# Output units of a two-layer hybrid decoder without overlap, and the last one in two halves of 256 columns

## The chip, the cores and the metric

The kernel runs on one core of one Trainium2 chip. The metric is the device time of one execution in microseconds (us); lower is better. The core's engines are named as in the profile: PE (TensorE matmul), DVE (VectorE), ACT (ScalarE), POOL (GpSimd) and SP (SyncE, which issues nearly all transfers).

## What is computed

Two layers run over one sequence of 512 tokens of width 1024, in float32. The reference, cut:

```python
def hybrid_layer(x, w_in, w_out, g_pre, g_post, lb, g_head, sinks):
    h = rms_norm(x, g_pre)
    proj = jnp.einsum('bsd,de->bse', h, w_in)                       # 1024 -> 6400
    q_h, f_h, i_h, z_h, q_a, k_a, v_a, z_a = jnp.split(proj, SPLIT_POINTS, axis=-1)
    o_h = hgrn2(q_h, f_h, i_h, lb)                                  # gated linear recurrence, 8 heads of 128
    o_h = rms_norm(o_h, g_head).reshape(B, S, HG_WIDTH) * jax.nn.silu(z_h)
    o_a = sliding_window_attention(rotary(q_a), rotary(k_a), v_a, sinks) * jax.nn.silu(z_a)
    y = jnp.einsum('bse,ed->bsd', jnp.concatenate([o_h, o_a], axis=-1), w_out)   # 2048 -> 1024
    return x + rms_norm(y, g_post)

def reference(x, ...):
    for l in range(DEPTH):                                          # DEPTH = 2
        x = hybrid_layer(x, w_in[l], w_out[l], ...)
    return x
```

The change is in the last lines of the layer: the product with `w_out`, the norm of its result `y`, and the sum with `x`. What follows in layer 0 is the norm at the start of layer 1.

## The kernel before

**Products and units.** Every large product is made of three matmuls, on operands split into a high and a low part (`whi`, `wlo` for weights; `hhi`, `hlo` for the normed input; `ops` for both parts of the gated branch outputs). `products` lists them. A *unit* (`Unit`) is one PSUM tile of a product, called `pj`, of 128 tokens (a *token tile*, `tt`, 0 to 3) by 512 columns. It has a number of steps, one per 128 rows of contraction, and each step is three matmuls (line 240). Three `pj` tiles exist.

**The order of units.** `enqueue` puts the units of a product in one queue, `units`, for both layers ahead of time; `step` issues one step. At most two units are active at a time, and their steps alternate: a second unit starts when the one active has at most half of its steps left. Only the key/value product (`fresh`) runs its units alone. When a unit has made its last step, its `evac` is called, which writes the instructions that take the result out of PSUM. `later` keeps work to be written a number of steps on; `ensure` writes it at once if a unit needs it.

**The output product.** Its weights come in four slabs: `a0`, `a1`, `h0`, `h1`, by 512 rows of the 2048. Each slab has 8 units, 4 token tiles by 2 column halves (`ch`) of 512, of 4 steps each. `wo_stream` queues them; the results of the four slabs are added up in the SBUF tiles `y` (line 786 for the first, line 789 for the others). The slab `h1` is the last of its layer, and its units go token tile by token tile. It follows the gate slab `ZH+1`, whose units have 8 steps; the transposes at line 770 turn that gate's result into `ops`.

**After the last product of a token tile** `final` runs. For column half 0: the square sum on ACT (line 819) and the product with `g_post` on POOL, in place (line 821). For column half 1: the square sum on ACT, the product with `g_post` on DVE (line 824, tile `s`), then `rstd2`: the two sums and a constant added on DVE (line 296), the power -1/2 on POOL (line 298, tile `r`); then for each half the scaling and sum with `x` on DVE (line 827, tile `a`) and the transfer from the SP queue (line 828), to `x_mid` in layer 0 and to the output in layer 1.

**The hand-over to layer 1.** In layer 0, `final` ends with `pre_norm`, the next layer's norm of that token tile: the squares of `a` on ACT (line 331, written to `hlo`), the weighing on DVE (`xg`, line 344), `rstd2` again, and a diagonal matrix of `r` on DVE (line 347, `z` in the profile). 18 steps later (`DEFER`) the transposes on PE against that diagonal (line 352) go into two of three PSUM tiles, `sc`, that take turns; ACT copies them out as `hhi` (line 357) and DVE as `hlo` (line 361). Layer 1's first product, keys and values (128 by 256 per unit), needs them.

**What sets the order.** The kernel's Python writes the instructions in one stream. A scheduler then places each engine's instructions by priority and dependence, so the order on an engine follows when work was written. Instructions wrapped in `pin`, and those under `tc.high_priority(200)` (the last additions into `y`), are treated apart. Within an engine the placed order is kept at run time.

Of the kernel before, what the change touches and what calls it, by code (L numbers as in the profile page):

```python
# [10 lines left out]
F32 = mybir.dt.float32  # L11
F32R = mybir.dt.float32r
U8 = mybir.dt.uint8
AF = mybir.ActivationFunctionType
ALU = mybir.AluOpType
# [5 lines left out]
NT = SEQ // 128  # L21
# [44 lines left out]
def hybrid_kernel(ctx: ExitStack, tc: tile.TileContext, x, wkv, win, wout, g_pre, g_post, lbp, ghead, sinks,  # L66
                  ident_c, cos_f, sin_f, cos_t, sin_t, masks_c, out):
    nc = tc.nc
    P = 128
# [5 lines left out]
    sm = ctx.enter_context(tc.tile_pool(name="sm", bufs=4))  # L75
# [6 lines left out]
    def pj():  # L82
        return ps.tile([P, 512], F32, tag="pj", name="pj", bufs=PJ)
# [8 lines left out]
    def ac():  # L92
        return ps.tile([P, 512], F32, tag="ac", name="ac", bufs=8 - PJ - SC)

    def tmp(tag, dt=F32, n=1):

        t = tp.tile([P, n, 512] if n > 1 else [P, 512], dt, tag=tag, name=tag, bufs=TB[tag])
        return t
# [6 lines left out]
    x_mid = dr.tile([SEQ, D_MODEL], F32, name="x_mid")  # L105
# [18 lines left out]
    for l in range(1, DEPTH):  # L124
        i = plan_order.index((l, "kv"))
# [35 lines left out]
    def w_conv(n):  # L161
        w_load(n)
        while state["conv"] < min(n, len(pieces)):
            i = state["conv"]
            if state["limit"] is not None and i >= state["limit"]:
                return
            if i in kv_pieces and kv_pieces[i] not in kv_room:
                return
            w_load(i + RAW_BUFS)
            v = raws.pop(i)  # L170
            if i in kv_pieces:
                hi, lo = (big.tile([P, 512], F32R, tag="v", name="wkv", bufs=8) for _ in range(2))
            else:
                hi = wp.tile([P, 512], F32R, tag="whi", name="whi")
                lo = wp.tile([P, 512], F32R, tag="wlo", name="wlo")
            keep = pin if i in in_turn else lambda ins: ins
            keep(nc.scalar.copy(hi, v))  # L177
            keep((nc.gpsimd if i in on_pool and i % 2 else nc.vector).tensor_tensor(lo, v, hi.bitcast(F32), op=ALU.subtract))  # L178
            conv[i] = (hi, lo)
            state["conv"] += 1  # L180
# [5 lines left out]
    def products(ks, fresh):  # L186
        if not fresh:
            return [(k, i, j) for k in ks for i, j in EACH]
        return [(k, i, j) for i, j in ((0, 0), (0, 1), (1, 0)) for k in ks]
# [8 lines left out]
    def run_first():  # L198
        _, key, fn = waiting.pop(0)
        fn()  # L200
        emitted.add(key)

    def ensure(key):
        while key not in emitted:
            run_first()
# [3 lines left out]
    class Unit:  # L209
        def __init__(self, key, ks, sta, mov, evac, needs, ncol):  # L210
            self.key, self.ks, self.sta, self.mov, self.evac, self.needs, self.ncol = key, list(ks), sta, mov, evac, needs, ncol
            self.i = 0
            self.fresh = key[0] == "kv"
            self.list = products(self.ks, self.fresh)

    units, active, turn, slab_steps, slab_done = deque(), [], [0], {}, {}

    def enqueue(key, specs, ncol=512):

        for ks, sta, mov, evac, needs in specs:  # L220
            units.append(Unit(key, ks, sta, mov, evac, needs, ncol))
            slab_steps[key] = slab_steps.get(key, 0) + len(units[-1].ks)
            slab_done.setdefault(key, 0)

    def step():
        if not active or (len(active) == 1 and units and not active[0].fresh and not units[0].fresh
                          and 2 * (len(active[0].ks) - active[0].i) <= len(active[0].ks)):
            u = units.popleft()
            first, n = slab_first[u.key]
            w_conv(first + n)  # L230
            u.w = [conv[first + j] for j in range(n)]
            for key in u.needs:
                ensure(key)
            u.o = pj()[:, 0:u.ncol]
            active.append(u)
        u = active[turn[0] % len(active)]
        turn[0] += 1
        for n in range(3 * u.i, 3 * u.i + 3):
            k, i, j = u.list[n]
            nc.tensor.matmul(u.o, lhsT=u.sta(k, u.w)[i], rhs=u.mov(k, u.w)[j], start=(n == 0), stop=(n == len(u.list) - 1))  # L240
        u.i += 1
        for e in waiting:
            e[0] -= 1
        while waiting and waiting[0][0] <= 0:
            run_first()
        slab_done[u.key] += 1
        first, n = slab_first[u.key]
        w_conv(ahead.get(u.key, first + n) + slab_done[u.key] * KT // slab_steps[u.key] + LEAD)
        if u.i == len(u.ks):
            active.remove(u)  # L250
            u.evac(u.o)
# [4 lines left out]
    def through(key):  # L256
        while slab_done[key] < slab_steps[key]:
            step()
            yield 1.0
# [41 lines left out]
    def halves(tag):  # L301
        t = tmp(tag, n=2)
        return [t[:, 0], t[:, 1]]

    def load_g(g):
        t = halves("b")
        for c in range(2):
            nc.sync.dma_start(t[c], g[c * 512:(c + 1) * 512].partition_broadcast(P))
        return t
# [70 lines left out]
    def diagonals():  # L380
        return tmp("z1").rearrange("p (n t) -> p n t", n=NT)

    def new_hT():
        return (hp.tile([P, KT, SEQ], F32R, tag="hhi", name="hhi"), hp.tile([P, KT, SEQ], F32R, tag="hlo", name="hlo"))


    def layer(l, last):
# [391 lines left out]
        yt = {}  # L779

        def wo_stream(b, s, final=None):
            def evac(o, tt, ch):
                if (b, s) == ("a", 0):
                    if ch == 0:
                        yt[tt] = big.tile([P, 2, 512], F32, tag="oy", name="y", bufs=6)
                    nc.scalar.copy(yt[tt][:, ch], o)
                else:
                    with tc.high_priority(200 if final else 0):
                        nc.vector.tensor_tensor(yt[tt][:, ch], o, yt[tt][:, ch], op=ALU.add)
                if final is not None:  # L790
                    final(tt, ch)

            enqueue(("out", l, f"{b}{s}"),
                    [(range(4 * ch, 4 * ch + 4), lambda k, w, tt=tt: tuple(t[:, k % 4, tt * P:(tt + 1) * P] for t in ops_t[b, s]),
                      lambda k, w: w[k], lambda o, tt=tt, ch=ch: evac(o, tt, ch), [("o", l, b, s, tt)])
                     for tt, ch in ([(tt, ch) for tt in range(NT) for ch in range(2)] if final else
                                    [(tt, ch) for ch in range(2) for tt in range(NT)])])


        hT2 = {}  # L800

        def final(tt, ch):
            if ch == 0:
                if tt == 0:
                    hT2["gpost"] = load_g(g_post[l])
                    if not last:
                        hT2["gpre"] = [ac() for _ in range(2)]
                        for c, t in enumerate(load_g(g_pre[l + 1])):
                            nc.scalar.copy(hT2["gpre"][c], t)
                        hT2["dg"] = diagonals()  # L810
                        state["limit"] = slab_first["in", l + 1, QA][0] + 2
                        hT[l + 1] = new_hT()
                hT2["x"] = halves("a")
                for c in range(2):
                    nc.sync.dma_start(hT2["x"][c], (x if l == 0 else x_mid)[tt * P:(tt + 1) * P, c * 512:(c + 1) * 512])
                hT2["ss"] = sm.tile([P, 2], F32, tag="ss", name="ss")
            xt, ss, y = hT2["x"], hT2["ss"], yt[tt]
            junk = tmp("u")
            nc.scalar.activation(junk, y[:, ch], AF.Square, scale=1.0 / 32.0, accum_out=ss[:, ch:ch + 1])
            if ch == 0:  # L820
                nc.gpsimd.tensor_tensor(y[:, 0], y[:, 0], hT2["gpost"][0], op=ALU.mult)
                return
            yg = tmp("s")
            nc.vector.tensor_tensor(yg, y[:, 1], hT2["gpost"][1], op=ALU.mult)
            r = rstd2(ss)
            for c, v in ((0, y[:, 0]), (1, yg)):
                nc.vector.scalar_tensor_tensor(xt[c], v, r, xt[c], op0=ALU.mult, op1=ALU.add)
                nc.sync.dma_start((out if last else x_mid)[tt * P:(tt + 1) * P, c * 512:(c + 1) * 512], xt[c])
            if not last:
                pre_norm(tt, xt, hT2["gpre"], hT[l + 1], ("h", l + 1, tt), hT2["dg"], DEFER)  # L830

# [72 lines left out]
    m, n = head[0], head[1]  # L904
# [141 lines left out]
```

## Time and profile before

| | |
|---|---|
| median of 3 runs | 951.08 us (949.64 to 951.56) |
| the profiled execution, its own time | 947.43 us |
| its span, first to last instruction | 945.3 us |
| granted TensorE clock | 0.998 |
| end of layer 0's last output product (last matmul starts) | 474.63 us |
| start of layer 1's first 512-column product | 493.76 us |
| last matmul starts | 937.07 us |
| last scaling on DVE starts | 941.32 us |

Times of instructions are counted from the span's start. Rows of the timeline give the start, the duration, the engine, the line of the code, the operation, and what is written from what; a bracket gives the engine's idle time ahead of it and what ended that. PE rows overlap, since a matmul's row reaches to its modelled end while the next already runs; the distance between starts is the pace. The tiles of one name are not told apart there (`s` is the tile at line 824 and also the small sum at line 296, told apart by 128x512 and 128x1).

### The profile page before, as it was taken

Reading aid. Unit: us, or ns where it says so; the run is one execution under the profiler, and the core shown is the slowest. Engines: PE = TensorE matmul, PEld = TensorE weight load, DVE = VectorE, ACT = ScalarE, POOL = GpSimd, SP = SyncE. Lnnn points to the kernel's source line nnn. Section 1 sums busy time; section 2 is a strip of 40 time slices with the busy share of each in tenths; the row PEclk is TensorE's granted clock in tenths of the full one; section 3 lists DMA queues with packets and bytes.
Section 4 is the critical chain, followed back from the end, with each engine's and each line's share of the span. In section 5 each row is a group of like instructions: output and inputs, shape, how many; then the busy total and the mean of one; then the engine's idle time right before and its main releaser. Section 6 shows DMA issues by size and latency. Waiting matters only on the chain.

```text
span 945.3 us, 19154 instructions
## 1 busy us (share of the span) xinstructions
PE 918.9 (97%) x7286; PEld 757.0 (80%) x7286; DVE 679.6 (72%) x1328; ACT 471.9 (50%) x1098; POOL 267.9 (28%) x285
## 2 busy tenths in 40 slices
PE   8999998999999999999999989989999999999996
PEld 6887787778878788788888877877787887887885
DVE  5787869796767685865776688778867668749546
ACT  4434656837464462334453266676463635415242
POOL 2232444422231221221222344433413213113102
PEclk9999999999999999999999999999999999999999
DMA  6475523132222333333445836123223233323313
GB/s 221 135 224 160 168 61 90 56 92 68 79 79 80 89 113 90 111 89 94 132 144 170 234 77 179 57 67 89 70 67 90 69 89 95 119 63 97 89 34 134
DMA packets 56432, 100.83 MB, mean 107 GB/s; under 512 B 6418, under 2 KB 8850, under 8 KB 56340
## 3 DMA queue, kind: packets, MB, share of 16 engines
q1 hardware_dynamic: 56192, 99.53, 35.7%
q8 instruction: 58, 0.95, 0.4%
q14 instruction: 34, 0.28, 0.1%
q10 hardware_dynamic: 148, 0.07, 0.0%
HBM read 87.00 MB, written 12.58 MB: 105 GB/s over the span
## 4 chain that ended last, share of the span: by engine, by line
PE 77%; DVE 10%; ACT 5%; issue 4%; POOL 2%; DMA 1%; SPq 0%; DVEq 0%; POOLq 0%; ACTq 0%
PE pj L240 64%; DVE wlo L178 3%; PE sc L653 2%; ACT s L512 2%; PE ac L722 2%; PE sc L498 1%; PE ac L710 1%; PE ac L551 1%; PE ac L725 1%; PE sc L352 1%; DVE oa L557 1%; ACT whi L177 1%; PE sc L770 1%; DVE mx L503 1%; DVE sc L502 1%
## 5 line engine op out<-in xcount | busy, mean ns | idle before, releaser
L177 ACT CAST whi<-raw 128x512 fp32r<-128x512 f32 x256 | 157.7, 620 | 183.6 <-PE pj L240 161.0
L178 DVE TENSOR_TENSOR wlo<-raw,whi 128x512 fp32r<-128x512 f32 x249 | 189.5, 767 | 56.3 <-ACT whi L177 54.4
L240 PE MATMUL pj<-hhi,wlo 128*128 128x512 f32 x512 | 205.5, 401 | 0.0
L240 PE MATMUL pj<-hhi,whi 128*128 128x512 f32 x512 | 200.0, 391 | 0.0
L240 PE MATMUL pj<-hlo,whi 128*128 128x512 f32 x512 | 199.7, 390 | 0.0
L240 PE MATMUL pj<-whi,ops 128*128 128x512 f32 x512 | 173.6, 398 | 0.0
L240 PEld LDWEIGHTS pj<-hhi,whi 128*128 128x128 f32 x512 | 96.1, 188 | 21.0
L240 PEld LDWEIGHTS pj<-whi,ops 128*128 128x128 f32 x512 | 96.1, 188 | 19.9
L240 PEld LDWEIGHTS pj<-hhi,wlo 128*128 128x128 f32 x512 | 96.2, 188 | 19.0
L240 PEld LDWEIGHTS pj<-hlo,whi 128*128 128x128 f32 x512 | 96.3, 188 | 18.2
L240 PE MATMUL pj<-whi,hlo 128*128 128x512 f32 x256 | 103.9, 406 | 0.0
L240 PE MATMUL pj<-whi,hhi 128*128 128x512 f32 x256 | 100.3, 392 | 0.0
L240 PE MATMUL pj<-wlo,hhi 128*128 128x512 f32 x256 | 100.2, 391 | 0.0
L240 PE MATMUL pj<-wlo,ops 128*128 128x512 f32 x256 | 99.7, 389 | 0.0
L671 POOL TENSOR_TENSOR k<-k,tot 128x256 f32<-128x256 f32 x80 | 65.2, 833 | 109.7 <-PE sc L653 64.3
L670 DVE TENSOR_TENSOR q<-q,tot 128x256 f32<-128x256 f32 x80 | 47.8, 625 | 15.6 <-PE sc L653 10.1
L512 ACT ACTIVATE s<-sc,negm 128x128 f32<-128x128 f32 x128 | 45.6, 369 | 25.0 <-DVE negm L506 22.9
L240 PEld LDWEIGHTS pj<-whi,hhi 128*128 128x128 f32 x256 | 48.1, 188 | 10.1
L240 PEld LDWEIGHTS pj<-wlo,ops 128*128 128x128 f32 x256 | 48.2, 188 | 9.0
L240 PEld LDWEIGHTS pj<-whi,hlo 128*128 128x128 f32 x256 | 48.2, 188 | 8.0
L519 POOL TENSOR_TENSOR s<-s,sums 128x512 f32<-128x512 f32 x32 | 33.4, 1043 | 74.5 <-DVE sums L517 37.6
L240 PEld LDWEIGHTS pj<-wlo,hhi 128*128 128x128 f32 x256 | 48.3, 189 | 7.7
(178 smaller groups left out, 1440.2 us busy)
## 6 DMA issues: line engine op xcount, KB each, us to landing
raw<-in_win_dram SPq DMA_DIRECT2D x192, 256.0 KB, 2.7
raw<-in_wout_dram SPq DMA_DIRECT2D x64, 256.0 KB, 2.7
stack<-rot SPq DMA_DIRECT2D x16, 512.0 KB, 4.6
qs<-stack SPq DMA_DIRECT2D x32, 256.0 KB, 4.9
a<-in_x_dram SPq DMA_DIRECT2D x12, 256.0 KB, 3.4
raw<-in_wkv_dram SPq DMA_DIRECT2D x8, 256.0 KB, 4.2
x_mid<-a SPq DMA_DIRECT2D x8, 256.0 KB, 3.4
a<-x_mid SPq DMA_DIRECT2D x8, 256.0 KB, 3.6
```

The lines of the kernel that those rows point to most:

```text
L177: keep(nc.scalar.copy(hi, v))
L178: keep((nc.gpsimd if i in on_pool and i % 2 else nc.vector).tensor_tensor(lo, v, hi.bitcast(F32), op=ALU.subtract))
L240: nc.tensor.matmul(u.o, lhsT=u.sta(k, u.w)[i], rhs=u.mov(k, u.w)[j], start=(n == 0), stop=(n == len(u.list) - 1))
L352: pin(nc.tensor.matmul(o[:, j * P:(j + 1) * P], lhsT=self.xg[:, c, j * P:(j + 1) * P], rhs=self.dg[:, self.tt], start=True, stop=True))
L498: pin(nc.tensor.matmul(S[:, h * 256:(h + 1) * 256], lhsT=q[:, 2 * hp_ + h, t_], rhs=kst[v][p][:, (n - 1) * P:(n + 1) * P], start=(h == 0 a ...
L502: nc.vector.copy_predicated(Sv[:, :, P:2 * P], am2, Sv[:, :, 0:P])
L512: nc.scalar.activation(pt[:, h * P:(h + 1) * P], cur[h], AF.Exp, bias=negm[:, h:h + 1], scale=SCALE, accum_out=sums[:, h:h + 1])
L519: nc.gpsimd.tensor_tensor(pv, pv, sums.unsqueeze(2).broadcast_to([P, 4, P]), op=ALU.mult)
L653: pin(nc.tensor.matmul(L[32 * b:32 * b + 32, c:c + 16], lhsT=k[:, o_:o_ + 32], rhs=qv[:, blk:blk + qu, 1, :], start=True, stop=True, tile_ ...
L670: nc.vector.tensor_tensor(qv[:, :, 1, :], qv[:, :, 1, :], tv[:, :, 0].unsqueeze(2).broadcast_to([P, nb, hh]), op=ALU.mult)
L671: nc.gpsimd.tensor_tensor(kv_[:, :, 0, :], kv_[:, :, 0, :], tv[:, :, 1].unsqueeze(2).broadcast_to([P, nb, hh]), op=ALU.mult)
L722: pin(nc.tensor.matmul(O[:, c], lhsT=A[:, c], rhs=vs(j, n), start=(n == 0), stop=False))
```

## The change

Units of the slab `h1`, of both layers, are `alone`, as the key/value units were: none starts beside them, and they start beside none. In the last layer the last unit of the slab (token tile 3, column half 1) is replaced by two units of 256 columns each. The additions into `y` and the square sums go by these halves; the sums of column half 0 and of the first 256 columns are added by one DVE instruction of one column, so that `rstd2` still adds two numbers. The last token tile's scaling goes in three parts (512, 256 and 256 columns), and the transfer of the second part is issued from ACT's queue, the others from SP's.

```diff
@@ class Unit
             self.fresh = key[0] == "kv"
+            self.alone = self.fresh or key[2] == "h1"
@@ def enqueue
-        for ks, sta, mov, evac, needs in specs:
-            units.append(Unit(key, ks, sta, mov, evac, needs, ncol))
+        for ks, sta, mov, evac, needs, *own in specs:
+            units.append(Unit(key, ks, sta, mov, evac, needs, own[0] if own else ncol))
@@ def step
-        if not active or (len(active) == 1 and units and not active[0].fresh and not units[0].fresh
+        if not active or (len(active) == 1 and units and not active[0].alone and not units[0].alone
                           and 2 * (len(active[0].ks) - active[0].i) <= len(active[0].ks)):
@@ def wo_stream
-                    with tc.high_priority(200 if final else 0):
-                        nc.vector.tensor_tensor(yt[tt][:, ch], o, yt[tt][:, ch], op=ALU.add)
+                    y = yt[tt][:, ch, c0:c0 + n]
+                    with tc.high_priority(200 if final else 0):
+                        nc.vector.tensor_tensor(y, o, y, op=ALU.add)
...
+            if final:
+                todo = [(tt, ch, 0, 512) for tt in range(NT) for ch in range(2)]
+                if last:
+                    todo[-1:] = [(NT - 1, 1, 0, 256), (NT - 1, 1, 256, 256)]
+            else:
+                todo = [(tt, ch, 0, 512) for ch in range(2) for tt in range(NT)]
@@ def final
-        def final(tt, ch):
+        def final(tt, ch, c0, n):
+            split = n < 512
...
+            if c0:
+                hT2["ss"] = sm.tile([P, 2], F32, tag="ss", name="ss")
+                nc.vector.tensor_tensor(hT2["ss"][:, 0:1], ss[:, 0:1], ss[:, 1:2], op=ALU.add)
+                ss = hT2["ss"]
             junk = tmp("u")
-            nc.scalar.activation(junk, y[:, ch], AF.Square, scale=1.0 / 32.0, accum_out=ss[:, ch:ch + 1])
+            nc.scalar.activation(junk[:, 0:n], y[:, ch, c0:c0 + n], AF.Square, scale=1.0 / 32.0, accum_out=ss[:, ch:ch + 1])
...
-            yg = tmp("s")
-            nc.vector.tensor_tensor(yg, y[:, 1], hT2["gpost"][1], op=ALU.mult)
+            if not c0:
+                hT2["yg"] = tmp("s")
+            yg = hT2["yg"]
+            nc.vector.tensor_tensor(yg[:, c0:c0 + n], y[:, 1, c0:c0 + n], hT2["gpost"][1][:, c0:c0 + n], op=ALU.mult)
+            if split and not c0:
+                return
             r = rstd2(ss)
-            for c, v in ((0, y[:, 0]), (1, yg)):
-                nc.vector.scalar_tensor_tensor(xt[c], v, r, xt[c], op0=ALU.mult, op1=ALU.add)
-                nc.sync.dma_start((out if last else x_mid)[tt * P:(tt + 1) * P, c * 512:(c + 1) * 512], xt[c])
+            parts = [(0, y[:, 0], 0, 512)] + [(1, yg, e, n) for e in range(0, 512, n)]
+            for i, (c, v, e, w) in enumerate(parts):
+                xs = xt[c][:, e:e + w]
+                nc.vector.scalar_tensor_tensor(xs, v[:, e:e + w], r, xs, op0=ALU.mult, op1=ALU.add)
+                (nc.scalar if split and i == 1 else nc.sync).dma_start(
+                    (out if last else x_mid)[tt * P:(tt + 1) * P, c * 512 + e:c * 512 + e + w], xs)
```

More of the change, by code (lines that the diff above doesn't have):

```diff
@@ L781, in wo_stream, with evac @@
         def wo_stream(b, s, final=None):
-            def evac(o, tt, ch):
+            def evac(o, tt, ch, c0, n):
                 if (b, s) == ("a", 0):
@@ L787, in evac @@
                 else:
+                    y = yt[tt][:, ch, c0:c0 + n]
                     with tc.high_priority(200 if final else 0):
-                        nc.vector.tensor_tensor(yt[tt][:, ch], o, yt[tt][:, ch], op=ALU.add)
+                        nc.vector.tensor_tensor(y, o, y, op=ALU.add)
                 if final is not None:
-                    final(tt, ch)
+                    final(tt, ch, c0, n)
+            if final:
[4 more added lines that the diff above has]
+                todo = [(tt, ch, 0, 512) for ch in range(2) for tt in range(NT)]
             enqueue(("out", l, f"{b}{s}"),
                     [(range(4 * ch, 4 * ch + 4), lambda k, w, tt=tt: tuple(t[:, k % 4, tt * P:(tt + 1) * P] for t in ops_t[b, s]),
-                      lambda k, w: w[k], lambda o, tt=tt, ch=ch: evac(o, tt, ch), [("o", l, b, s, tt)])
-                     for tt, ch in ([(tt, ch) for tt in range(NT) for ch in range(2)] if final else
-                                    [(tt, ch) for ch in range(2) for tt in range(NT)])])
+                      lambda k, w, c0=c0, n=n: tuple(t[:, c0:c0 + n] for t in w[k]),
+                      lambda o, e=(tt, ch, c0, n): evac(o, *e), [("o", l, b, s, tt)], n)
+                     for tt, ch, c0, n in todo])
         hT2 = {}
-        def final(tt, ch):
+        def final(tt, ch, c0, n):
+            split = n < 512
             if ch == 0:
```

## The prediction, made before the changed kernel was run

> **What bounds the kernel now.** I read the page first, for where the end is set, then the order of time on each engine at the two places that the change touches: the hand-over from layer 0 to layer 1, and the last 20 us.
>
> ```profile
> PE 918.9 (97%) x7286; PEld 757.0 (80%) x7286; DVE 679.6 (72%) x1328; ACT 471.9 (50%) x1098; POOL 267.9 (28%) x285
> PE 77%; DVE 10%; ACT 5%; issue 4%; POOL 2%; DMA 1%; SPq 0%; DVEq 0%; POOLq 0%; ACTq 0%
> ```
>
> Those are the busy times and the chain that ended last. TensorE is both busy and on the chain, so a change pays only where it removes TensorE work or a stall of TensorE, or shortens the head or tail. This one removes no work. TensorE in order of time at the hand-over (L352 are the transposes of the next layer's input, one token tile each; the 128x256 matmuls are layer 1's key/value product):
>
> ```profile
> 469.65 1.95 PE L352 MATMUL sc<-z,xg 128*128 128x128 f32 x16
> 475.97 2.35 PE L352 MATMUL sc<-z,xg 128*128 128x128 f32 x16
> 481.03 1.06 PE L352 MATMUL sc<-z,xg 128*128 128x128 f32 x8
> 483.44 1.16 PE L352 MATMUL sc<-z,xg 128*128 128x128 f32 x8 [1.36 <-DVE hlo L361]
> 490.88 2.08 PE L240 MATMUL pj<-wkv,hhi 128*128 128x256 f32 x16
> 492.80 1.12 PE L240 MATMUL pj<-wkv,hlo 128*128 128x256 f32 x8
> 493.76 0.40 PE L240 MATMUL pj<-hhi,wlo 128*128 128x512 f32 x1
> 494.46 0.40 PE L240 MATMUL pj<-hhi,wlo 128*128 128x512 f32 x1
> 497.19 0.39 PE L240 MATMUL pj<-hhi,wlo 128*128 128x512 f32 x1
> ```
>
> Here TensorE is not free: the second group of token tile 2 (483.44) waits 1.36 us for DVE's hlo, which empties the PSUM bank it needs; tile 1's transposes are also stretched (2.35 against 1.95). So the hand-over hangs on the vector chain of the four token tiles, and what that chain loses, TensorE loses. From 493.76 on layer 1's first 512-column products run, and everything after it moves with it. DVE there (y: a product added out of PSUM; a lone s<-ss: the sum of squares; a: the scaling; z: the diagonal of the next norm; xg, hlo: the next norm's input):
>
> ```profile
> 457.62 0.75 DVE L773 SCALAR_TENSOR_TENSOR ops<-sc,gh,ops 128x512 fp32r<-128x512 f32 x1 [1.78 <-ACT ops L772]
> 458.29 0.68 DVE L789 TENSOR_TENSOR y<-pj,y 128x512 f32<-128x512 f32 x1
> 463.77 0.68 DVE L789 TENSOR_TENSOR y<-pj,y 128x512 f32<-128x512 f32 x1
> 465.63 0.29 DVE L347 TENSOR_SCALAR z<-ident,r 128x128 f32<-128x128 f32 x1 [0.45 <-POOL r L298]
> 469.77 0.68 DVE L789 TENSOR_TENSOR y<-pj,y 128x512 f32<-128x512 f32 x1
> 471.56 0.29 DVE L347 TENSOR_SCALAR z<-ident,r 128x128 f32<-128x128 f32 x1 [0.44 <-POOL r L298]
> 471.76 0.69 DVE L824 TENSOR_TENSOR s<-y,b 128x512 f32<-128x512 f32 x1
> 472.36 0.15 DVE L296 SCALAR_TENSOR_TENSOR s<-ss 128x1 f32<-128x1 f32 x1
> 480.10 0.75 DVE L827 SCALAR_TENSOR_TENSOR a<-y,r,a 128x512 f32<-128x512 f32 x1 [0.72 <-POOL r L298]
> 482.70 0.69 DVE L361 TENSOR_TENSOR hlo<-sc,hhi 128x512 fp32r<-128x512 f32 x1
> 468.89 1.29 POOL L821 TENSOR_TENSOR y<-y,b 128x512 f32<-128x512 f32 x1 [2.28 <-ACT u L819]
> 470.60 0.93 POOL L298 TENSOR_TENSOR r<-s,mhalf 128x1 f32<-128x1 f32 x1 [0.41 <-DVE s L296]
> ```
>
> DVE hardly waits before z: it has put the next tile's second y (463.77, 469.77) ahead of it. POOL has to finish a 1.3 us product before the r that z needs. The tail:
>
> ```profile
> 937.07 0.39 PE L240 MATMUL pj<-whi,ops 128*128 128x512 f32 x1
> 937.50 0.69 DVE L789 TENSOR_TENSOR y<-pj,y 128x512 f32<-128x512 f32 x1 [0.28 <-PE pj L240]
> 938.11 1.27 POOL L821 TENSOR_TENSOR y<-y,b 128x512 f32<-128x512 f32 x1 [2.94 <-ACT u L819]
> 938.23 1.70 DVE L824 TENSOR_TENSOR s<-y,b 128x512 f32<-128x512 f32 x1
> 938.28 0.63 ACT L819 ACTIVATE u<-y 128x512 f32<-128x512 f32 x1 [0.25 <-DVE y L789]
> 938.82 0.18 ACT L819 ACTIVATION_READ_ACCUMULATOR u<-y 128x1 f32 x1
> 939.85 0.15 DVE L296 SCALAR_TENSOR_TENSOR s<-ss 128x1 f32<-128x1 f32 x1
> 940.65 0.75 DVE L827 SCALAR_TENSOR_TENSOR a<-y,r,a 128x512 f32<-128x512 f32 x1 [0.66 <-POOL r L298]
> 941.43 0.99 SPq L828 DMA_DIRECT2D out_dram<-a  x2
> 942.20:943.80 1.60, 0.00 (x0) 0.00 (x0) 0.00 (x0) 0.00 (x0) 0.00 (x0) 0.50 0.88 328
> SPq L1042 <- DMA out_dram<-a: 1.8, 1, 1.8
> ```
>
> From TensorE's end (937.46) to the first scaling are 3.2 us of vector work, then 4.65 us of scaling, output transfer and closing.
>
> **The change, part by part.**
>
> *Units run alone in both layers.* TensorE issues the same 512-column matmuls, so its own sum changes by 0. A unit is 4 steps of 3 matmuls; 12 of them stand between 494.46 and 497.19, 2.73 us or 0.227 each. The last ZH unit no longer shares with the first h1 units, so ZH ends 9 matmuls, 2.04 us, earlier, and each h1 unit but the last one step, 0.68 us. By itself that helps. But the order of DVE and ACT moves with it, and in layer 0 the vector chain, not TensorE, sets the pace. DVE, layer 0, token tiles 0 and 1 (a_51xx are tile 0's scalings, y_2801 tile 1's two products, z1 tile 0's diagonal), before:
>
> ```order
> L827 SCALAR_TENSOR_TENSOR a_5162<-y_2780,r1_5195,a_5162 128x512
> L789 TENSOR_TENSOR y_2801<-pj_5172,y_2801 128x512
> L827 SCALAR_TENSOR_TENSOR a_5162<-s_5191,r1_5195,a_5162 128x512
> L344 TENSOR_TENSOR xg_5201<-a_5162,ac_5152 128x512
> L344 TENSOR_TENSOR xg_5201<-a_5162,ac_5153 128x512
> L789 TENSOR_TENSOR y_2801<-pj_5215,y_2801 128x512
> L296 SCALAR_TENSOR_TENSOR s1_5207<-ss_5202 128x1
> L824 TENSOR_TENSOR s_5249<-y_2801,b_5149 128x512
> L347 TENSOR_SCALAR z1_5159<-ident_82,r1_5209 128x128
> L296 SCALAR_TENSOR_TENSOR s1_5251<-ss_5229 128x1
> ```
>
> and after:
>
> ```order
> L848 SCALAR_TENSOR_TENSOR a_5158<-y_2780,r1_5191,a_5158 128x512
> L848 SCALAR_TENSOR_TENSOR a_5158<-s_5187,r1_5191,a_5158 128x512
> L791 TENSOR_TENSOR y_2801<-pj_5208,y_2801 128x512
> L345 TENSOR_TENSOR xg_5197<-a_5158,ac_5148 128x512
> L345 TENSOR_TENSOR xg_5197<-a_5158,ac_5149 128x512
> L297 SCALAR_TENSOR_TENSOR s1_5203<-ss_5198 128x1
> L348 TENSOR_SCALAR z1_5155<-ident_82,r1_5205 128x128
> L791 TENSOR_TENSOR y_2801<-pj_5229,y_2801 128x512
> L841 TENSOR_TENSOR s_5245<-y_2801,b_5145 128x512
> L297 SCALAR_TENSOR_TENSOR s1_5247<-ss_5225 128x1
> ```
>
> The second y and its product now stand behind the diagonal z, which waits for POOL; the same happens once more, for tiles 1 and 2. I carried the rows' durations through the new order, each engine in its own order (the same reckoning of the old order meets the old rows within 0.4 us).
> - Tile 0: y, 458.29 before because ops (457.62) held it, follows its matmuls at about 456.7; the lead is 1.5 us.
> - Tile 1: POOL's product starts when ACT has done two squares of the norm and then tile 1's own, 462.0, and runs 1.3; r is ready at 463.95; z at 464.0; so y at 464.2 against 463.77. The lead is gone.
> - Tile 2: POOL's product 469.5 to 470.8, z 471.4, y 471.6 against 469.77. Its product with the weights, a weight conversion that stood at 470.43 in the old wait, and the sum s follow at 473.55 against 472.36: +1.2.
> - Tile 3: its second y now stands behind hlo of tile 0, itself behind a z: scaling at 481.5 against 480.10, +1.4.
>
> Then ACT. Around tile 1's hhi it stood, before (hlo here is the square of tile 3's output, which waits for the scalings):
>
> ```order
> L819 ACTIVATE u_5371,ss_5357<-y_2853 128x512
> L357 CAST hhi_5160<-sc0_78 128x4x128
> L357 CAST hhi_5160<-sc1_79 128x4x128
> L331 ACTIVATE hlo_5161,ss_5384<-a_5354 128x4x128 x2
> L398 COPY rkv_5445<-pj_5394 128x256
> ```
>
> and after:
>
> ```order
> L834 ACTIVATE u_5371,ss_5353<-y_2853 128x512
> L358 CAST hhi_5156<-sc0_78 128x4x128
> L332 ACTIVATE hlo_5157,ss_5384<-a_5350 128x4x128
> L358 CAST hhi_5156<-sc1_79 128x4x128
> L332 ACTIVATE hlo_5157,ss_5384<-a_5350 128x4x128
> L399 COPY rkv_5445<-pj_5394 128x256
> ```
>
> A square that waits for tile 3 has got in front of tile 1's second hhi, which the key/value matmuls need; the second square ends about 0.2 us later for it. DVE's hlo of 482.70 comes at 484.3 (+1.6), the waiting transposes start at 485.05 instead of 483.44 (+1.6), and three more 256-column matmuls stand behind them than before (3 x 0.12 = 0.36). Sum for the hand-over: **+2.0 us**. All later waits of layer 1 start from here, and I find none that would take it up: ACT's next conversions stand behind the last hhi, which moves by the same amount. Bounds: if only the last hold-up (s at +1.2, no more) counts, 1.2; if tile 3's square and the extra wait of hhi also cost, 2.8.
>
> *The halves.* 24 matmuls of 256 columns instead of 12 of 512. Price of 256: 16 start at 490.88 and the next row at 492.80, so 0.120 each. 24 x 0.120 - 2.73 = +0.15 us. TensorE ends at 937.6.
>
> *The vector tail.* DVE, last token tile (y and s by halves; ss adds the first two sums), after:
>
> ```order
> L791 TENSOR_TENSOR y_8009<-pj_10407,y_8009 128x512
> L791 TENSOR_TENSOR y_8009<-pj_10428,y_8009 128x256
> L841 TENSOR_TENSOR s_10444<-y_8009,b_10271 128x256
> L831 TENSOR_TENSOR ss_10460<-ss_10424 128x1
> L791 TENSOR_TENSOR y_8009<-pj_10446,y_8009 128x256
> L841 TENSOR_TENSOR s_10444<-y_8009,b_10271 128x256
> L297 SCALAR_TENSOR_TENSOR s1_10465<-ss_10460 128x1
> L848 SCALAR_TENSOR_TENSOR a_10421<-y_8009,r1_10467,a_10421 128x512
> L848 SCALAR_TENSOR_TENSOR a_10421<-s_10444,r1_10467,a_10421 128x256 x2
> ```
>
> Before, one y stood in place of the two halves, with one s, s1 and two scalings. Prices of 256 columns:
>
> ```profile
> 494.70 0.42 DVE L415 TENSOR_TENSOR a<-rkv,kcos 128x256 f32<-128x256 f32 x1
> 482.18 0.35 ACT L398 COPY rkv<-pj 128x256 f32<-128x256 f32 x1
> ident<-in_ident_dram ACTq DMA_DIRECT2D x1, 64.0 KB, 3.9
> ```
>
> Tile 2's scalings still hold the first y of tile 3 until 935.8. Its square ends on ACT at 937.3, the first half's square at 937.7, so the ss add waits until 937.8 and holds the second half's y, ready at 937.6, until 937.9. That y ends 938.3, its square 938.9. POOL's product (937.4 to 938.7) holds the second s until 938.7; it ends about 939.1. Sum at 939.0, r, first scaling at 939.8 against 940.65: **-0.85 us**, with -0.5 if POOL costs more and -1.1 if DVE's add waits for nothing.
> The hold by POOL is read from the two rows at 938.11 and 938.23: s took 1.70 beside POOL, against 0.69 in its undisturbed rows (471.76 is one). The Trainium skill, page SBUF — State Buffer, section Who interferes with whom, says that a DVE instruction with two SBUF inputs and a GpSimd instruction that reads SBUF exclude each other, the first one holding the port to its end; the trace agrees (1.70 against 0.69). Without that rule the sum s would start on ACT's word at 939.0 all the same, so the sum by it differs by under 0.1.
>
> *Transfers.* The same 512 KB leave after the first scaling. In 942.2 to 943.8 the 16 engines are 0.88 busy at 328 GB/s, so the second transfer starts as the first ends; a smaller last part has nothing to gain, one more issue, on ACT, is on an idle engine. Bounds: -0.35 (half of 256 KB at about 370 GB/s less behind the last issue) and +1.45 (the only transfer from ACT's queue took 3.9 to land; issued 1.1 after the first scaling it would land at 5.0, against 3.55 now: the issues end at 942.4, the wait of 1.8 at 944.2). I take 0, from the nearest row, the window. The Trainium skill, page DMA: Bandwidth & Descriptors, section Issuing engines are not separate DMA queues, says that transfers from different issuing engines end on the same 16 engines and only issue time is saved; by it the second queue is worth 0, by the opposite rule 0.35.
>
> **Sum.** +2.0 - 0.85 + 0 = +1.15, the +0.15 being inside the tail's times. The profiled execution took 947.43 (span 945.3 and 2.1 around it): 948.6. The median of the runs, 951.08, stands 3.65 above that execution, so the median becomes **952.2 us**.
>
> **Rivals.**
> - *Faster: the lead of tile 0 survives.* If z finds its r on POOL (DVE idle before z under 0.2 us), each tile runs 1.4 us ahead, hlo comes before TensorE asks, and the 1.36 and 0.4 us of waiting go: -1.7 - 0.85, so 948.5. Against it: in the new order POOL's 1.3 us product still stands ahead of that r, as at 468.89 and 470.60, and z has nothing ahead of it to cover it. It decides if the wait before z is short.
> - *The hand-over is neutral.* DVE's lateness meets slack and only the tail counts: 950.2. Against it: TensorE waited 1.36 us on exactly that chain, so there is no slack.
> - *ACT's queue lands late* on top of the forecast: +1.45, 953.7. For it: the one row of 3.9. Against it: that row lies at the start of the program, among many loads.
>
> **How the numbers follow.** Forecast 0.62 (own range 951.2 to 953.4), tile 0's lead survives 0.08, neutral hand-over 0.15, late ACT queue 0.15. What a measurement of this kernel can tell is 0.2%, or 1.9 us (949.2 to 953.0). Slower: 0.13 of the late queue and 0.14 of the forecast's upper part, 0.27. Faster: 0.06 of the first rival and 0.02 of the neutral one, 0.08. Within: 0.65. The range 950.0 to 954.0 holds the forecast, most of the neutral case and of the late queue; it leaves out the first rival.
>
> **What would show it.** In layer 0 DVE should wait 1.5 us or so before z twice, and TensorE should wait over 1 us for hhi of tile 1 and again at tile 2's transposes, with layer 1's first 512-column matmul about 2.0 later than 493.76. The last 256-column matmuls should stand 0.12 apart, the ss add should wait on ACT, and the first scaling should follow TensorE's end by 2.2 instead of 3.2 us. The prediction falls if layer 1 starts at or before 493.8, or if the last transfer lands over 4 us after the first scaling.

## The result and the profile after

The changed kernel takes 952.11 us (median of 11 runs, 950.29 to 955.03), the kernel before beside it 949.64 (946.81 to 951.56): a ratio of 1.0032, 95% interval 1.0019 to 1.0045. That is about 3.0 us slower, 1.8 to 4.3, so most of the interval lies beyond the 1.9 us (0.2%) that the prediction called telling. The profiled execution took 954.63, its span 952.6. Its granted clock was 0.991, that of the one before 0.998.

The clock matters for all that follows. Executions of one kernel differ by it: over the 251 executions of the 14 kernels here, a straight line with an offset for each kernel and one slope for all gives 0.67 us for each 0.001 of clock. The offsets, against the kernel before, are the "equal clock" differences below (95%: +-0.3). The changed kernel's is +1.90. The rest of the 3.0 goes with the mean clock of its eleven executions, 0.9935 against 0.9949 for the kernel before in the batches of the experiments, and whether that belongs to the change is open.

These offsets pool the kernel before over three batches of runs, each on a chip of its own, and at equal clock it stood 0.46 us (+-0.2) higher in the batch of l0_only, l1_only, z_pool and l1_alone_whole than in the other two. With an offset for each batch as well, a kernel is compared with the kernel before of its own batch; that is the fairer difference, and the table of times gives both. For the change itself only the pooled one can be had, since the clocks of the kernel before that ran beside it are not on record.

The page of the changed kernel, busy times and the chain that ended last:

```profile
PE 925.4 (97%) x7298; PEld 763.4 (80%) x7298; DVE 681.4 (72%) x1332; ACT 471.7 (50%) x1100; POOL 267.1 (28%) x285
PE 78%; DVE 9%; ACT 5%; issue 5%; POOL 2%; POOLq 0%; DVEq 0%; ACTq 0%
```

Nothing changed its rank; the 6.5 us more of PE are about what the clock makes of 918.9 (0.998/0.991: 6.5). For the shift at the hand-over the two traces need a common zero: the second of layer 0's groups of transposes out of ident, which lies ahead of every instruction that the change moves. First the kernel before, then the changed one, TensorE in order of time:

```profile
444.44 0.60 PE L770 MATMUL sc<-ident,z 128*128 128x128 f32 x4
...
484.35 1.07 PE L240 MATMUL pj<-wkv,hhi 128*128 128x256 f32 x7
```

```profile
446.90 0.60 PE L771 MATMUL sc<-ident,z 128*128 128x128 f32 x4
...
479.09 0.51 PE L241 MATMUL pj<-wkv,hhi 128*128 128x256 f32 x2 [1.15 <-ACT hhi L358]
480.99 1.16 PE L353 MATMUL sc<-z,xg 128*128 128x128 f32 x8 [0.50 <-DVE hlo L362]
486.31 0.51 PE L241 MATMUL pj<-wkv,hhi 128*128 128x256 f32 x2 [1.54 <-ACT hhi L358]
486.65 2.23 PE L353 MATMUL sc<-z,xg 128*128 128x128 f32 x16
488.64 1.44 PE L241 MATMUL pj<-wkv,hhi 128*128 128x256 f32 x10
498.42 0.40 PE L241 MATMUL pj<-hhi,wlo 128*128 128x512 f32 x1
```

The drift ahead of the change is 446.90 - 444.44 = 2.46 us. Layer 1's first 512-column product stood at 493.76 and now stands at 498.42 - 2.46 = 495.96: the hand-over costs **+2.20 us**. TensorE's waits there are 1.15, 0.50 and 1.54, where it had one of 1.36. The transposes of tile 2 (486.65), at which it had waited, now start without one: the wait that ends last is for tile 1's hhi, just ahead of them. The rows by which this happened, DVE and POOL of the changed kernel around the diagonals of tiles 0 and 1:

```profile
464.67 1.29 POOL L836 TENSOR_TENSOR y<-y,b 128x512 f32<-128x512 f32 x1 [2.94 <-ACT u L834]
464.88 1.09 DVE L297 SCALAR_TENSOR_TENSOR s<-ss 128x1 f32<-128x1 f32 x1
466.65 0.29 DVE L348 TENSOR_SCALAR z<-ident,r 128x128 f32<-128x128 f32 x1 [0.67 <-POOL r L299]
466.85 0.68 DVE L791 TENSOR_TENSOR y<-pj,y 128x512 f32<-128x512 f32 x1
474.05 0.29 DVE L348 TENSOR_SCALAR z<-ident,r 128x128 f32<-128x128 f32 x1 [0.66 <-POOL r L299]
474.26 0.68 DVE L791 TENSOR_TENSOR y<-pj,y 128x512 f32<-128x512 f32 x1
```

Between 464.88 and 466.65 DVE does no useful work but a sum of one column: 1.09 us of it is that sum, held until POOL's product ends (464.67 + 1.29 = 465.96), and 0.67 is the wait for r. The second y stands behind all of it; it comes at 464.39 and, in tile 2, at 471.80 with the drift off, against 463.77 and 469.77 before. The tail of the changed kernel:

```profile
944.69 0.28 PE L241 MATMUL pj<-whi,ops 128*128 128x256 f32 x1
944.79 1.26 POOL L836 TENSOR_TENSOR y<-y,b 128x512 f32<-128x512 f32 x1 [2.94 <-ACT u L834]
945.28 0.78 DVE L831 TENSOR_TENSOR ss<-ss 128x1 f32<-128x1 f32 x1 [0.60 <-ACT u L834]
945.99 0.41 DVE L791 TENSOR_TENSOR y<-pj,y 128x256 f32<-128x256 f32 x1
946.43 0.43 DVE L841 TENSOR_TENSOR s<-y,b 128x256 f32<-128x256 f32 x1
947.03 0.16 DVE L297 SCALAR_TENSOR_TENSOR s<-ss 128x1 f32<-128x1 f32 x1 [0.17 <-ACT u L834]
947.85 0.75 DVE L848 SCALAR_TENSOR_TENSOR a<-y,r,a 128x512 f32<-128x512 f32 x1 [0.66 <-POOL r L299]
949.03 0.38 ACTq L849 DMA_DIRECT2D out_dram<-a  x1
```

TensorE ends at 944.97, the first scaling starts at 947.85: 2.88 us later, where it was 3.19 (937.46 to 940.65). The added ss sum, one column, takes 0.78 us and ends with POOL's product (946.05); the y of the second half, whose matmuls were done at 944.97, starts behind it. From the first scaling to the span's end it is 4.75, before 4.65. The 16 DMA engines are 0.93 busy from 949.4 to 951.0 and idle from there to the end, so the last bytes, ACT's too, have moved 3.15 us after the first scaling.

### The profile page after: what moved, and what is told of

It reads as the page before. It is cut to its first block, busy times and chain, and to the rows that moved or that the text cites. A ratio compares the mean times of both kernels' runs of the same rounds, so it can differ in the third digit from the quotient of the medians.

```text
span 952.6 us, 19186 instructions
## 1 busy us (share of the span) xinstructions
PE 925.4 (97%) x7298; PEld 763.4 (80%) x7298; DVE 681.4 (72%) x1332; ACT 471.7 (50%) x1100; POOL 267.1 (28%) x285
## 4 chain that ended last, share of the span: by engine, by line
PE 78%; DVE 9%; ACT 5%; issue 5%; POOL 2%; POOLq 0%; DVEq 0%; ACTq 0%
PE pj L241 64%; DVE wlo L178 3%; PE sc L654 2%; ACT s L513 2%; PE sc L499 2%; PE ac L723 1%; PE sc L353 1%; PE ac L711 1%; PE ac L552 1%; PE ac L726 1%; ACT whi L177 1%; DVE oa L558 1%; PE sc L771 1%; DVE a L848 1%; PE sc L526 1%
## 5 line engine op out<-in xcount | busy, mean ns | idle before, releaser
L241 PE MATMUL pj<-whi,ops 128*128 128x512 f32 (+1 forms) x520 | 173.2, 395 | 0.0
L241 PE MATMUL pj<-wlo,ops 128*128 128x512 f32 (+1 forms) x260 | 100.4, 386 | 0.0
```

## The experiments

Each kernel was run against the kernel before on the same chip. Two tables hold what the traces and runs gave; the texts after them say what each run was for. The hand-over, in us: the zero, the first key/value row after tile 2's transposes, how many 256-column matmuls stand behind those transposes before the first 512-column product, that product's start, and its shift (start less 493.76, less the difference of the zeros):

| kernel | zero | after tile 2's transposes | matmuls behind | first 512 product | shift |
|---|---|---|---|---|---|
| before | 444.44 | 484.35 | 63 | 493.76 | |
| the change | 446.90 | 488.64 | 66 | 498.42 | +2.20 |
| l0_only | 447.54 | 489.27 | 66 | 499.05 | +2.19 |
| l1_only | 445.63 | 485.54 | 63 | 494.95 | 0.00 |
| l1_alone_whole | 444.56 | 484.48 | 63 | 493.89 | +0.01 |
| z_pool | 445.87 | 486.00 | 66 | 495.78 | +0.59 |
| defer17 | 444.20 | 485.81 | 69 | 495.95 | +2.43 |
| z_pool_defer17 | 445.44 | 485.42 | 69 | 495.56 | +0.80 |
| both_whole | 444.29 | 484.27 | 69 | 494.40 | +0.79 |
| defer20 | 444.45 | 487.98 | 60 | 497.03 | +3.26 |
| layer1_add_defer20 | 447.05 | 489.20 | 57 | 497.90 | +1.53 |
| both_add_defer20 | 445.47 | 486.97 | 60 | 496.03 | +1.24 |
| add_on_act | 444.40 | 484.31 | 63 | 493.71 | -0.01 |
| one_queue | 445.80 | 485.71 | 63 | 495.12 | 0.00 |

In each row the shift is the lateness of the third column plus 0.12 us for each matmul more than 63 (the change: 488.64 - 2.46 - 484.35 = 1.83, and 3 x 0.12 = 0.36: 2.19). From tile 2's transposes on TensorE has no slack. The four kernels that leave layer 0 as before and `DEFER` at 18 have a shift of -0.01 to +0.01, though their profiles' clocks differ (0.994 to 0.998): so far can one profile's shift be trusted.

The tail and the times:

| kernel | TensorE's end to first scaling | first scaling to span's end | ratio to before, 95% | at equal clock, pooled | at equal clock, own batch | by the trace |
|---|---|---|---|---|---|---|
| before | 3.19 | 4.65 | | | | |
| the change | 2.88 | 4.75 | 1.0032 (1.0019 to 1.0045) | +1.90 | | +2.14 |
| l0_only | 3.18 | 4.64 | 1.0032 (1.0016 to 1.0048) | +2.42 | +2.12 | +2.17 |
| l1_only | 2.86 | 4.76 | 0.9988 (0.9975 to 1.0000) | -0.06 | -0.37 | -0.07 |
| l1_alone_whole | 2.52 | 4.70 | 0.9985 (0.9973 to 0.9998) | -0.36 | -0.68 | -0.61 |
| one_queue | 2.88 | 4.77 | 0.9989 (0.9977 to 1.0001) | -0.48 | -0.33 | -0.04 |
| add_on_act | 2.07 | 4.79 | 0.9979 (0.9967 to 0.9992) | -0.96 | -0.82 | -0.84 |
| z_pool | 2.91 | 4.83 | 0.9996 (0.9985 to 1.0007) | +0.15 | -0.15 | +0.64 |
| defer17 | 2.87 | 4.76 | 1.0029 (1.0016 to 1.0041) | +2.07 | +2.22 | +2.37 |
| z_pool_defer17 | 2.88 | 4.77 | 1.0011 (1.0001 to 1.0021) | +0.05 | +0.20 | +0.76 |
| both_whole | 2.49 | 4.65 | 0.9997 (0.9984 to 1.0010) | -0.21 | -0.07 | +0.09 |
| defer20 | 2.86 | 4.77 | 1.0028 (1.0016 to 1.0040) | +2.86 | +3.01 | +3.20 |
| layer1_add_defer20 | 2.07 | 4.83 | 1.0009 (1.0001 to 1.0018) | +0.48 | +0.64 | +0.74 |
| both_add_defer20 | 2.07 | 4.77 | 1.0008 (0.9997 to 1.0018) | +0.11 | +0.28 | +0.39 |

The last column adds the shift at the hand-over, the two columns of the tail less those of before, and 0.15 where the last unit is in halves.

**Layer 0 alone, layer 1 alone.**

```diff
-            self.alone = self.fresh or key[2] == "h1"
+            self.alone = self.fresh or key[1:] == (0, "h1")          # l0_only, its last unit whole
+            self.alone = self.fresh or key[1:] == (DEPTH - 1, "h1")  # l1_only, in halves
```

> Units of h1 alone in layer 0 only; layer 1 as before, its last unit whole. Theory (the loss is the hand-over, where the next tile's second y stands behind a diagonal that waits for POOL): layer 1's first 512-column product 2.0 to 2.5 us later than 493.76 once the drift of the rows ahead is taken off, and the time +2.3 us over before; after TensorE's end all as before (3.2 us to the first scaling). Rival A (the loss is in layer 1 or in the tail): 0. Rival B (the loss is the granted clock, which follows the program as a whole): the waits of TensorE at the hand-over as before, and a lower clock.

> Units of h1 alone in layer 1 only, with the last unit in halves; layer 0 as before. Theory: the hand-over as before, and only the tail counts: -0.15 us by the rows of the changed kernel (2.88 against 3.19 from TensorE's end to the first scaling, and 0.15 more of matmuls), so the same as before within 0.5 us. By the prediction's tail: -0.85. Rival A (the loss is in layer 1 or in the tail): +2 to +3.

Layer 0's part alone costs +2.19 us in the trace and +2.42 at equal clock (+2.12 in its own batch), with the tail as it was; layer 1's part alone leaves the hand-over where it was and the time at -0.06 (-0.37). The loss is at the hand-over, and rivals A and B fall. The tail brings about what the trace of the change said, not the predicted -0.85.

**The last unit whole.** Layer 1 alone as above, and the list of units is not cut:

```diff
-                if last:
+                if False:
                     todo[-1:] = [(NT - 1, 1, 0, 256), (NT - 1, 1, 256, 256)]
```

> Units of h1 alone in layer 1 only, and the last unit whole, with its two scalings and transfers on one queue as before; layer 0 as before. Theory: nothing of the loss is here; within 0.5 us of before. Against the kernel with layer 1 alone in halves it should stand 0.15 us higher by the rows of the changed kernel, 0.85 higher by the prediction's tail. Rival A (running the units of layer 1 alone costs): +1 or more.

It is no slower than the halves, but faster if anything (0.30 at equal clock, inside the uncertainty of two such numbers). The trace of the tail says why:

```profile
937.19 0.39 PE L241 MATMUL pj<-whi,ops 128*128 128x512 f32 x1
937.56 1.27 POOL L836 TENSOR_TENSOR y<-y,b 128x512 f32<-128x512 f32 x1 [2.95 <-ACT u L834]
938.34 1.03 DVE L841 TENSOR_TENSOR s<-y,b 128x512 f32<-128x512 f32 x1
940.10 0.75 DVE L848 SCALAR_TENSOR_TENSOR a<-y,r,a 128x512 f32<-128x512 f32 x1 [0.66 <-POOL r L299]
```

The units ahead of the last end earlier when they run alone. Tile 2's second scaling, behind which tile 3's first y stands on DVE, starts at 935.31 instead of 935.87, and POOL's product starts as TensorE ends (937.56 against 937.58) instead of 0.65 later (938.11 against 937.46). The s beside it is held for 0.34 (1.03 against 0.69) instead of 1.01, and the first scaling comes 2.52 after TensorE's end. So the gain of the tail comes from running alone (0.67), and the halves as they are made here give 0.34 of it back, besides 0.15 of matmuls; that they do it through ss is tested below.

**The diagonal off DVE's queue.**

```diff
-        m.diag()
+        nc.gpsimd.tensor_scalar(m.dg[:, m.tt], ident, m.r, None, op0=ALU.mult)
```

> The whole change, but the diagonal z of the next norm is made by POOL, behind its own r, and no longer stands in DVE's queue. Theory (z on DVE, waiting for POOL, holds the next tile's second y): the cost of the hand-over goes; the first 512-column product of layer 1 comes at or before 493.8 with the drift taken off, the time is 0 to -2 us against before. Rival (the square of tile 3 ahead of the second hhi on ACT, or the lost overlap of the units, is what costs): it stays at +1.5 to +2.5.

```profile
463.85 1.10 DVE L297 SCALAR_TENSOR_TENSOR s<-ss 128x1 f32<-128x1 f32 x1
464.87 0.68 DVE L791 TENSOR_TENSOR y<-pj,y 128x512 f32<-128x512 f32 x1
...
483.67 0.50 PE L241 MATMUL pj<-wkv,hhi 128*128 128x256 f32 x2 [1.49 <-ACT hhi L358]
484.01 2.24 PE L353 MATMUL sc<-z,xg 128*128 128x128 f32 x16
```

On DVE, y now follows s at once: it comes at 463.44 and, in tile 2, at 470.04 with the drift off, 0.95 and 1.76 earlier than in the changed kernel. The small sum ahead of it is still held by POOL's product (1.10), so that hold alone does not cost the 2 us. Of the 2.20 at the hand-over 1.61 are gone and 0.59 stay, so the first 512-column product stands at 494.35 with the drift off, not at or before 493.8: the main cause is shown, but it is not the whole. What stays is 0.22 of lateness and 0.36 of matmuls behind the wait. The wait for hhi (1.49) is still there, which asked for the next pair of kernels.

**ACT's order.** One number of the program puts tile 1's second hhi ahead of tile 3's squares:

```diff
-DEFER = 18
+DEFER = 17
```

> The whole change, with the next norm's transposes issued 17 steps of the products after their input instead of 18: that alone puts tile 1's second hhi ahead of tile 3's squares on ACT, and leaves DVE's order as it is. Theory (two holds: 1.6 us from z behind POOL, 0.7 from the square ahead of the second hhi): TensorE's wait of 1.54 us for hhi goes, layer 1 starts 0.4 to 0.7 us earlier than in the changed kernel with the drift taken off, and the time is +0.9 to +1.2 over before at equal granted clock. Rival (ACT's order is only a symptom of the late scalings on DVE): the wait moves to another instruction and the start stays at +2.3, the time at +1.6.

> The whole change, with both remedies: z made by POOL, and 17 steps instead of 18. Theory: both holds are gone and the hand-over is neutral or better, first 512-column product of layer 1 at 493.2 to 493.8 with the drift taken off; against before at equal granted clock -0.4 (the tail alone) to -1.0. Rival (a third hold, such as POOL's slower diagonal, 1.1 to 1.6 us against 0.29 on DVE): it stays at +0.7, the time at +0.2.

```profile
478.29 1.16 PE L353 MATMUL sc<-z,xg 128*128 128x128 f32 x8 [2.26 <-DVE hlo L362]
484.90 1.16 PE L353 MATMUL sc<-z,xg 128*128 128x128 f32 x8 [1.69 <-DVE hlo L362]
```

These are the first of the two, TensorE. Its wait for hhi went, and 2.26 and 1.69 us of waiting for DVE's hlo took its place: the rival was right, ACT's order is a symptom. The shift did not fall but rose, +2.43 and with z on POOL +0.80: the lateness is 0.13 and 0.15 smaller, and three more matmuls stand behind the wait, 0.36. My theory of a second hold of 0.7 on ACT falls; what that square costs is about 0.15 by this pair. In the second kernel the rival's number came (+0.7), but not by a third hold: of the +0.80 only 0.07 is lateness, and 0.72 are the six matmuls more than before.

**More work ahead of the wait.** The other direction, 20 steps, in the change, in the best tail, and with z on POOL:

```diff
-DEFER = 18
+DEFER = 20
```

> The whole change, with the next norm's transposes issued 20 steps of the products after their input instead of 18. Six 256-column key/value matmuls (6 x 0.12 = 0.72 us) so move from behind the transposes of tile 2, where TensorE waits, to ahead of them; before, 63 of them stood behind, in the change 66, here 60. Theory (what the change costs at the hand-over is a late vector chain plus the matmuls that stand behind the wait, and more work ahead of the wait fills it): layer 1 starts 0.7 us earlier than in the changed kernel with the drift taken off, +1.6 instead of +2.3 against before; the time 0.7 below the changed kernel at equal clock, +0.9 to +1.1 over before. Rival (the wait moves on to hhi of the later tiles): within 0.2 us of the changed kernel.

> Layer 0's units as before, layer 1 alone and in halves with the sum of the first two partial squares on ACT, and 20 steps instead of 18. Before itself waits 1.36 us at tile 2's transposes; six matmuls fewer stand behind them. Theory: 0.7 us off the start of layer 1, on top of the -1.0 of the tail: -1.5 to -1.8 us against before at equal clock. Rival (key/value of tile 2 waits for its hhi, since its transposes come later): -0.8 to -1.1, the tail alone.

> The whole change with z made by POOL, 20 steps instead of 18, and the sum of the first two partial squares on ACT. Theory: the hand-over of z on POOL was +0.7 and loses 0.7; with the tail's -1.0 that is -0.8 to -1.1 us against before at equal clock. Rival: +0.7 stays at the hand-over, -0.3.

All three missed:

```profile
476.66 0.74 PE L241 MATMUL pj<-wkv,hhi 128*128 128x256 f32 x4 [1.63 <-ACT hhi L358]
478.37 1.22 PE L241 MATMUL pj<-wkv,hhi 128*128 128x256 f32 x8 [0.97 <-ACT hhi L358]
485.22 1.22 PE L241 MATMUL pj<-wkv,hhi 128*128 128x256 f32 x8 [1.93 <-ACT hhi L358]
```

These are the first of the three, TensorE. The transposes come later, and the key/value product of the same tile then waits for its hhi, three times. The rival of the first text (the wait moves on) was right, and it cost more than it said: +3.26 against +2.20. In the second, 0.72 of matmuls less stands against 2.24 of new lateness. By the trace's shift the place of the transposes is a narrow one: 17 and 20 both lose to 18. In time, 17 is not told apart from 18 (+2.07 against +1.90).

**The sum of one column, off DVE.** Layer 1 alone and in halves, and:

```diff
-                nc.vector.tensor_tensor(hT2["ss"][:, 0:1], ss[:, 0:1], ss[:, 1:2], op=ALU.add)
+                nc.scalar.activation(hT2["ss"][:, 0:1], ss[:, 0:1], AF.Identity, bias=ss[:, 1:2])
```

> Layer 0 as before; layer 1 alone and in halves, but the sum of the first two partial squares of the last tile is made on ACT instead of DVE. Theory (that sum of one column sits behind POOL's product on DVE and holds the second half's y by 0.7 us): y follows TensorE's end by 0.1 instead of 1.0, and the first scaling follows it by 2.2 to 2.5 us instead of 2.88, so 0.4 to 0.6 us under the kernel with DVE's sum. Rival (y only changes places with the second s, which waits for POOL's product anyway): 2.7 to 2.9, less than 0.2 gained.

```profile
937.26 0.28 PE L241 MATMUL pj<-whi,ops 128*128 128x256 f32 x1
937.34 1.26 POOL L836 TENSOR_TENSOR y<-y,b 128x512 f32<-128x512 f32 x1 [2.95 <-ACT u L834]
937.58 0.42 DVE L791 TENSOR_TENSOR y<-pj,y 128x256 f32<-128x256 f32 x1 [0.34 <-PE pj L241]
937.84 0.29 ACT L831 ACTIVATE ss<-ss 128x1 f32<-128x1 f32 x1
938.04 0.85 DVE L841 TENSOR_TENSOR s<-y,b 128x256 f32<-128x256 f32 x1
939.61 0.75 DVE L848 SCALAR_TENSOR_TENSOR a<-y,r,a 128x512 f32<-128x512 f32 x1 [0.66 <-POOL r L299]
```

The sum takes 0.29 on ACT beside the same product of POOL, y starts 0.04 after TensorE's end (937.54), and the first scaling follows by 2.07. Against the kernel with DVE's sum this is 0.79 in the trace, more than expected, and 0.90 at equal clock, or 0.45 by their own batches. The hold of that one sum, and not the halving itself, is what cost the tail. s, which cannot avoid POOL, is still held (0.85 against 0.43), but it has begun to wait earlier. This kernel, 947.61 us against 949.18 of before in its batch, has the lowest ratio of the study, 0.9979, and is faster than before and than the change; l1_alone_whole, 0.9985, is not told apart from it.

**One queue.** Layer 1 alone, in halves:

```diff
-                (nc.scalar if split and i == 1 else nc.sync).dma_start(
+                nc.sync.dma_start(
```

> Layer 0 as before, layer 1 alone and in halves, the three last transfers all issued by SP instead of one of them by ACT. Theory (the last transfers share the same 16 engines, and only issue time differs): from the first scaling to the end of the span 4.65 to 4.9 us against 4.75 with two queues; the time within 0.3 us of the kernel with two. Rival 1 (the second queue saves issue time on the path): +0.4 to +0.5, one more issue on SP behind the last scaling. Rival 2 (ACT's queue lands late): 0.5 or more faster with one queue.

From the first scaling to the end it takes 4.77 with one queue and 4.76 with two: the second queue is worth nothing here, as the theory said. The Trainium skill, page DMA: Bandwidth & Descriptors, section Issuing engines are not separate DMA queues, says that a second issuing engine saves only the time to issue; these two numbers agree that it gains nothing beyond that. At equal clock this kernel is 0.42 below the one with two queues, which the traces don't show; the two ran in different batches, and by their own batches they are 0.04 apart (-0.33 and -0.37).

**Both layers, the last unit whole** (z on POOL, 17 steps):

> Both remedies of the hand-over, units alone in both layers, and the last unit whole with its transfers on one queue as before. Theory: the tail of the whole unit run alone (first scaling 2.52 us after TensorE's end against 3.19: -0.65) and a neutral or better hand-over add up to -0.65 to -1.3 us against before at equal granted clock, the fastest so far. Rival (a third hold at the hand-over): 0.

The tail came as expected (2.49), and the hand-over kept 0.79, which eats it: -0.21 (-0.07 in its own batch). The rival's number was right, but what stays is again the six matmuls (0.72), not a third hold. Running layer 0's units alone pays in none of the forms tried.

**What stays open.** The column by the trace and the runs of the same batch agree within 0.3 us, which is the uncertainty of the runs, for all kernels but two. The two are the kernels with z on POOL that keep the change's tail: the trace gives +0.64 and +0.76, the runs -0.15 and +0.20. One profile each cannot say where these 0.6 to 0.8 us are. The 0.22 us of lateness that z_pool keeps is not traced to a cause either.

## Why the prediction was right or wrong

The time, 952.2, came within 0.1 us of the median, but partly by luck: it stood on 951.08, the median of 3 runs, which over 11 runs beside the change was 949.64. The forecast's own sum was +1.15, the measured move is +1.90 at equal clock and +3.0 as the runs fell. A base that stood 1.4 too high and a sum that came out too low made up for each other. Most of the chance (0.65) was on a move within 0.2%; what came lies at that bound or beyond it on the slow side, which had 0.27.

- *Hand-over, +2.0: right in mechanism, measured +2.20.* Of it 1.83 is tile 2's late transposes (forecast 1.6) and 0.36 the three matmuls behind them (forecast 0.36). With the drift of 2.46 off, the rows came: tile 0's y at 456.93 (forecast 456.7), tile 1's y at 464.39 (464.2), tile 2's at 471.80 (471.6), tile 3's scaling at 481.82 (481.5). The lead of 1.5 us was there (1.36) and was spent, as the step said, behind z. That z is the cause is shown by z_pool, for 1.61 of the 2.20. The last wait was not the one forecast: TensorE was to wait for DVE's hlo at tile 2's transposes (485.05) and waited for ACT's hhi just ahead of them instead (1.54). With ACT's order changed in defer17, the wait for hlo came in its place (1.69), so both carry the same lateness of DVE's chain.
- *DVE waits about 1.5 us before z, twice: right in size, wrong in look.* 0.67 shows as a wait, and some 0.9 hides inside a sum of one column that takes 1.09 instead of 0.15.
- *ACT's square ahead of hhi:* the wait for hhi over 1 us came, twice (1.15 for tile 0's, 1.54 for tile 1's). As a cause of its own the order is worth little, as the forecast had it (0.2; defer17 and its twin: 0.13 and 0.15).
- *Nothing later takes it up: right.* The shift at layer 1's start reached the end: l0_only ends like before, 2.1 to 2.4 later.
- *Halves, 0.12 us for each 256-column matmul: right.* The last ones in the trace stand 0.12 apart.
- *The vector tail, -0.85: the step that failed.* The matmuls' 0.15 taken in, the measured net is -0.16 (2.88 - 3.19 + 0.15). The step let the ss sum wait for ACT's square and then run 0.1; it waited as said but ran 0.78, until POOL's product ended, and held y. The same reckoning had applied POOL's hold to the 256-column s one line further down, and quoted for it the rule of the Trainium skill (page SBUF — State Buffer, section Who interferes with whom) that a DVE instruction with two SBUF inputs and a GpSimd instruction that reads SBUF exclude each other; ss has two SBUF inputs as well, and the trace agrees with the rule for one column as for 512. With that one sum on another engine the first scaling follows TensorE's end by 2.07, where the step forecast 2.2. POOL's product came where the step had it (0.18 ahead of TensorE's end, forecast 0.2), but the step did not say that this comes from running alone: the whole unit run alone already has 2.52.
- *Transfers, 0: right* within 0.1: +0.10 for three parts, 0.01 between two queues and one. ACT's queue did not land late (the DMA engines are idle from 3.15 after the first scaling, where the sign asked for over 4); that rival falls.
- *The faster rival* fell by its own test: z waits 0.67, not under 0.2. *The neutral hand-over* falls by +2.20.

## What to carry to other kernels

Before an instruction of a busy engine's queue is put ahead of another, look what it waits for: here a diagonal of 0.3 us put a 0.7 us sum out of PSUM off by 0.95 us in one token tile and by 1.76 in the next, because its operand came from a third engine. Price even the smallest added instruction by the engine that it may be shut out by, not by its columns. And change places one layer at a time: the same edit lost 2.2 us in the layer with a successor and, with the last unit whole, gained 0.36 at equal clock (0.68 in its own batch) in the layer without one.

## What the hardware showed that was not expected

A DVE instruction on one column with two SBUF inputs took 0.78 us (ss at 945.28), 1.09 and 1.10 us (s at 464.88, and at 463.85 with z on POOL) beside a product on POOL, and 0.15 to 0.16 without one; each time it ended within 0.02 us of POOL's product (465.97 against 465.96, 946.06 against 946.05, 464.95 against 464.94). The same holds in each of the 12 such rows in the traces of the changed kernel, l0_only, l1_only, z_pool and defer17, which took 0.78 to 1.10. In the rows these read as busy time, not as waiting. ACT's sum of the same one column took 0.29 beside POOL.

Two more rows of the kernel before bear on this:

```profile
468.57 1.28 DVE L344 TENSOR_TENSOR xg<-a,ac 128x512 f32<-128x512 f32 x2
464.60 1.00 POOL L298 TENSOR_TENSOR r<-s,mhalf 128x1 f32<-128x1 f32 x1 [0.41 <-DVE s L296]
```

The weighing xg takes one of its two inputs (`ac`) from PSUM: two of them took 1.28 us beside POOL's product (468.89 to 470.18), and 1.28 without one (481.43). And the hold goes the other way too: POOL's r took 1.00 and 0.93 (at 464.60 and 470.60) when DVE had just begun an instruction with two SBUF inputs (at 464.49 and 470.43), and 0.54 to 0.55 otherwise in that stretch.
